# x read also in feature layout, its norm spread by small matmuls, and the modulation products moved to TensorE

## Chip, cores, metric

One core of one Trainium2 chip. The metric is the device time of one execution in microseconds, as the median of several runs. Engines are named as in the profile: PE (TensorE, matmuls), PEld (its weight loads), DVE (VectorE), ACT (ScalarE), POOL (GpSimd), SP (the engine that issues most DMAs).

## The reference, cut to what matters

```python
cond = jax.nn.silu(c)
mod = cond @ w_ada[l] + b_ada[l]                      # c: 1024, w_ada: 1024 x 3072
shift, scale, gate = jnp.split(mod, 3, axis=-1)
h = rmsnorm(x, norm_w[l]) * (1.0 + scale[:, None]) + shift[:, None]   # x: 2048 x 1024
u = h @ w_in[l]
a_x, a_g, hg_q, hg_f, hg_i, hg_g, ssd_z, ssd_xbc, ssd_dt = jnp.split(u, split_points, axis=-1)
...  # three branches: RG-LRU (ya), HGRN2 (yb), SSD (yc), each over 2048 tokens
y = jnp.concatenate([ya, yb, yc], axis=-1) @ w_out[l]
x = x + gate[:, None] * y
return rmsnorm(x, final_norm_w)
```

`rmsnorm(x, w)` is `x * rsqrt(mean(x*x, features) + eps) * w`.

## The kernel before

The 2048 tokens are cut into four blocks `tb` of 512 and the 1024 features into eight tiles `k` of 128. The normalised and modulated input is kept as eight `ht` tiles per block, 128 features by 512 tokens, each as a rounded high part and a low part (`hi`, `lo`), and each weight block likewise, so that one 128x512 projection tile is three matmuls. Blocks 0 and 1 are projected first (half 0), blocks 2 and 3 later (half 1).

*How an h tile is made.* `load_x` reads x as tokens by features. `norm_stats` squares it on ACT with a running sum, and takes root and reciprocal to `st`, one column per group of 128 tokens. `norm_scale` multiplies each x tile by its column of `st`, mostly on DVE. `h_tile` transposes four 128x128 pieces on PE (`ps_xt`), ACT applies scale and shift (`hf`, from the columns `gsc` of feature tile k), DVE rounds to the high part (a cast) and DVE or POOL subtracts for the low part.

*How `gsc` is made.* `mod_dma(j)` loads the shift and scale columns of w_ada that belong to feature tile j (`wta`). `mod_acc` multiplies and accumulates eight pieces on DVE into `macc`. `mod_col` sums `macc` over the partitions with a matmul by ones (`psm`), and DVE makes two columns of `gsc` in three small operations.

*The order of the opening* (blocks 0 and 1) is written by hand in a word list, `PROG`: D j loads, A j (part) multiplies, C j is `mod_col`, X loads x, S takes statistics, N scales x, H block k makes an h tile (a last `v` puts the low part on DVE instead of POOL), w and W load and split the first three weight blocks, M block k is nine matmuls of one h tile with them (`ps_f`, `ps_q`, `ps_g`), K makes constants, B starts the branches. PE runs in the order in which the code issues. A scheduler orders the other engines when the program is built, each engine then runs its queue strictly in order.

*The middle.* In the last pass of half 0 (loop index `i` 0 to 3; `ps_lx`, `ps_lg` are the projections of the RG-LRU, `ps_r`, `ps_i` its gate matmuls, `l_r` its scan, `l_gs` its output) x of block 2 is loaded at `i == 2` and scaled by the generator `norm_gen`; at `i == 3` x of block 3 is loaded and scaled in line, and `h_build(2)` makes block 2's h tiles between the projections. Half 1 starts with `ps_v` of block 2, woven with `h_build(3)`. Small tiles of 128x512 (`xt`, `xsq`, `macc`, `wta`, `raw`, `hf`) share 34 slots, so a load can wait until a slot is free.

Of the kernel before, what the change touches and what calls it, by code (L numbers as in the profile page):

```python
# [30 lines left out]
for _name, _w in (("norm_w", 8), ("b_shift", 8), ("b_scale", 8), ("c", 8),  # L31
# [13 lines left out]
LW, HGW = 2, 20  # L45
BW = (4, 1)
L0 = 0.01


@with_exitstack  # L50
def trunk(ctx, tc, x, w_ada, w_in, w_out, wa, wx, cols, rows, ident_in,
          tri_in, masks_in, onehot_in, out):
    nc = tc.nc
    V, S, G, PE = nc.vector, nc.scalar, nc.gpsimd, nc.tensor
# [11 lines left out]
    def act(o, i, f, **kw):  # L66
        S.activation(o, i, f, **kw)  # L67

    def tt(e, o, a, b, op):
        e.tensor_tensor(o, a, b, op=op)  # L70
# [212 lines left out]
    def norm_stats(xs):
        st = tmp("xst", (P, 2, 4), bufs=2)
        for n in range(2):
            for i in range(4):
                sq = tmp("xsq", (P, TB), BF16, bufs=1)
                act(sq, xs[i][n], AF.Square, accum_out=st[:, n, i:i + 1])
        tt(V, st[:, 0], st[:, 0], st[:, 1], ADD)
        sact(st[:, 0], st[:, 0], AF.Sqrt, scale=1.0 / D, bias=epsc[:, 0:1])  # L290
        V.reciprocal(st[:, 0], st[:, 0])
        return st

    def norm_scale(xs, st, n, on_act=()):
        for i in range(4):
            if on_act is G:
                tt(G, xs[i][n], xs[i][n], st[:, 0, i:i + 1].to_broadcast([P, TB]), MUL)
            elif i in on_act:
                act(xs[i][n], xs[i][n], AF.Copy, scale=st[:, 0, i:i + 1])
            else:  # L300
                V.tensor_scalar(xs[i][n], xs[i][n], st[:, 0, i:i + 1], None, op0=MUL)

    def norm_x(xs, on_act=()):
        st = norm_stats(xs)
        for n in range(2):
            norm_scale(xs, st, n, on_act)

    def h_tile(xs, k, dep=None, lo=G):
        ht = hp.tile([P, 2, TB], F32R, tag="h", name="ht")
        ps = bank(ps_ms, "ms", "ps_xt")  # L310
        for i in range(4):
            d_ = PE.transpose(ps[:, i * P:(i + 1) * P], xs[i][k // 4][:, (k % 4) * P:(k % 4 + 1) * P], ident)
# [3 lines left out]
        V.tensor_copy(ht[:, 0], hf)  # L316
# [112 lines left out]
    def mod_dma(j):  # L429
        mws[j] = []  # L430
        for q in range(4):
            wt = tmp("wta", (P, 2, 2, P))
            for s in range(2):
                nc.sync.dma_start(wt[:, :, s], w_ada[q * 256:(q + 1) * 256, s * D + j * P:s * D + (j + 1) * P]
                                  .rearrange("(k p) c -> p k c", p=P))
            mws[j].append(wt)

    def mod_acc(j, part):
        if part == 0:
            mas[j] = tmp("macc").rearrange("p (s c) -> p s c", c=P)  # L440
        ma = mas[j]
        for q in (2 * part, 2 * part + 1):
            wt = mws[j][q]
            for k in range(2):
                kk = 2 * q + k
                if kk == 0:
                    V.tensor_scalar(ma[:, 0:2], wt[:, k], cond[:, 0:1], None, op0=MUL)
                else:
                    stt(ma[:, 0:2], wt[:, k], cond[:, kk:kk + 1], ma[:, 0:2], MUL, ADD)

    def mod_col(j):
        ma = mas.pop(j)
        psm = bank(ps_ms, "ms", "psm")
        for i in range(2):
            PE.matmul(psm[:, i:i + 1], ma[:, i], ones[:, 0:1], start=True, stop=True)
# [444 lines left out]
    for half in range(2):  # L900
# [4 lines left out]
        for p in range(2):  # L905
# [26 lines left out]
            if half == 0 and p == 0:  # L932
# [100 lines left out]
        for i in range(4):  # L1033
# [214 lines left out]
```

## Time and profile before

| | us |
|---|---|
| median of 3 runs | 1797.67 (1796.58 to 1798.63) |
| span of the profiled execution | 1793.9 |
| PE busy in it | 1712.6 (95%) |
| DVE, POOL, ACT busy | 1138.6, 835.9, 627.3 |

The profiled execution's span stands 3.8 us under the median of the timed runs; the runs are about 1 us apart from each other. A row of the timeline reads: start, duration, engine, line of the kernel, operation, written tile `<-` read tiles, shapes, number of instructions, and in brackets the idle time of that engine ahead of it with what ended it. PE's fp32 matmuls show as two records each, and the ends of matmuls are modelled, so the distance from one start to the next is the better measure of a PE row. A row of the waits reads: engine, tile and line that waited, what it waited for, us in total, times, longest.

### The profile page before, as it was taken

What the parts mean: (1) busy time and instruction counts of PE and PEld (TensorE: products, weight loads), DVE (VectorE), ACT (ScalarE), POOL (GpSimd) and SP (SyncE); (2) the same over time, 40 slices, a digit from 0 to 9 for tenths busy, and PEclk for the clock granted to TensorE, in tenths of its full rate; (3) what the DMA queues carried; (4) which work ended last, traced back from release to release, by engine and by line L of the source; (5) the groups of instructions that cost most, each with busy time, mean ns of one, the idle gap of its engine ahead of it and who ended that gap; (6) DMA issues with size and microseconds to landing.
All of it is one profiled execution on the core that took longest, in us unless ns stands there. A gap on an engine that the chain in (4) does not pass through costs nothing. (4 is left out here: it accounts for less than half of the span.)

```text
span 1793.9 us, 29607 instructions
## 1 busy us (share of the span) xinstructions
PE 1712.6 (95%) x11448; PEld 1363.9 (76%) x11448; DVE 1138.6 (63%) x2340; ACT 627.3 (35%) x1188; POOL 835.9 (47%) x682
## 2 busy tenths in 40 slices
PE   3899999999999999899999999999999799999998
PEld 2688877777777777787877777777777577888886
DVE  6944657788877856815655778868759745333333
ACT  5322323233333357622322334333355632222221
POOL 3433334265635655524234346545567645333334
PEclk9899999999999999999999999999999999999999
DMA  8611011111202132321111002211234353333332
GB/s 249 176 37 48 25 37 37 36 36 48 71 24 57 51 109 82 82 65 31 43 43 37 25 27 57 57 39 36 58 96 131 115 159 119 96 96 95 95 95 69
DMA packets 178988, 129.51 MB, mean 72 GB/s; under 512 B 13856, under 2 KB 153632, under 8 KB 178848
## 3 DMA queue, kind: packets, MB, share of 16 engines
q1 hardware_dynamic: 142512, 102.72, 20.1%
q10 hardware_dynamic: 33936, 17.04, 3.2%
q0 software_dynamic: 2400, 7.87, 1.1%
q8 instruction: 90, 1.47, 0.3%
q14 instruction: 50, 0.41, 0.1%
HBM read 102.43 MB, written 25.17 MB: 71 GB/s over the span
## 5 line engine op out<-in xcount | busy, mean ns | idle before, releaser
L1087 PE MATMUL po<-wo,yy 128*128 128x512 f32 x1512 | 355.1, 397 | 3.2 <-POOL yy L70 2.5
L1087 PEld LDWEIGHTS po<-wo,yy 128*128 128x128 f32 x1512 | 285.1, 189 | 73.0 <-POOL yy L70 2.9
L70 POOL TENSOR_TENSOR w<-raw,w 128x512 fp32r<-128x512 f32 x158 | 225.1, 1444 | 218.3 <-ACT w L67 218.2
L73 DVE SCALAR_TENSOR_TENSOR cacc<-craw,col,cacc 128x512 f32<-128x512 f32 x192 | 199.3, 1038 | 2.0
L324 PE MATMUL ps_x<-ht,w 128*128 128x512 f32 x768 | 196.3, 403 | 0.0
L324 PE MATMUL ps_z<-ht,w 128*128 128x512 f32 x768 | 192.7, 401 | 0.0
L324 PEld LDWEIGHTS ps_x<-ht,w 128*128 128x128 f32 x768 | 139.2, 188 | 38.6 <-issue 10.7
L324 PEld LDWEIGHTS ps_z<-ht,w 128*128 128x128 f32 x768 | 140.9, 188 | 34.5 <-issue 4.1
L70 POOL TENSOR_TENSOR hg_k<-hg_k,hg_t 128x256 f32<-128x256 f32 x80 | 58.9, 736 | 192.5 <-PE ps_sB L579 70.5
L73 DVE SCALAR_TENSOR_TENSOR o<-po,rstd,o 128x512 f32<-128x512 f32 x64 | 47.5, 750 | 118.8 <-PE po L1087 110.5
L324 PE MATMUL ps_f<-ht,w 128*128 128x512 f32 x384 | 105.9, 415 | 6.2 <-DVE ht L316 5.8
L330 PE MATMUL ps_v<-vw,ht 128*128 128x264 f32 x768 | 105.5, 292 | 4.6 <-DVE ht L70 4.6
L67 ACT ACTIVATE w<-raw 128x512 fp32r<-128x512 f32 x158 | 91.4, 624 | 47.7 <-PE ps_q L324 29.5
L324 PE MATMUL ps_bc<-ht,w 128*128 128x512 f32 x384 | 107.2, 413 | 0.0
L324 PE MATMUL ps_q<-ht,w 128*128 128x512 f32 x384 | 105.8, 412 | 0.0
L330 PEld LDWEIGHTS ps_v<-vw,ht 128*128 128x128 f32 x768 | 97.1, 191 | 8.0 <-DVE ht L70 5.5
L324 PE MATMUL ps_lx<-ht,w 128*128 128x512 f32 x384 | 101.4, 416 | 0.0
L70 POOL TENSOR_TENSOR s_ce<-s_ce,cacc 128x512 f32<-128x512 f32 x64 | 98.1, 1552 | 3.1 <-ACT s_ce L67 2.7
L70 POOL TENSOR_TENSOR o<-o,gate 128x512 f32<-128x512 f32 x32 | 43.0, 1351 | 117.7 <-DVE o L70 112.5
L324 PE MATMUL ps_lg<-ht,w 128*128 128x512 f32 x384 | 94.2, 398 | 0.0
L324 PE MATMUL ps_g<-ht,w 128*128 128x512 f32 x336 | 92.4, 408 | 0.0
L70 POOL TENSOR_TENSOR yy<-yr,yy 128x512 fp32r<-128x512 f32 x61 | 78.4, 1308 | 26.3 <-ACT yy L67 25.9
(248 smaller groups left out, 3060.5 us busy)
## 6 DMA issues: line engine op xcount, KB each, us to landing
raw<-in_w_in SPq DMA_DIRECT2D x176, 256.0 KB, 3.2
yr<-yscr SPq DMA_DIRECT2D x64, 256.0 KB, 2.9
wta<-in_w_ada SPq DMA_DIRECT2D x64, 128.0 KB, 3.0
xt<-in_x SPq DMA_DIRECT2D x32, 256.0 KB, 5.0
yscr<-cacc ACTq DMA_DIRECT2D x32, 256.0 KB, 2.3
rawo<-in_w_out SPq DMA_DIRECT2D x32, 256.0 KB, 3.4
xr<-in_x SPq DMA_DIRECT2D x32, 256.0 KB, 3.1
out<-o POOLq DMA_DIRECT2D x30, 256.0 KB, 4.4
```

Source lines behind the costliest of these rows:

```text
L67: S.activation(o, i, f, **kw)
L70: e.tensor_tensor(o, a, b, op=op)
L73: V.scalar_tensor_tensor(o, a, s, b, op0=op0, op1=op1)
L324: d_ = PE.matmul(ps, b.hl[wl][:, k, :], ht[:, hl, :], start=(k == 0 and n == 0), stop=(k == KT - 1 and n == 2))
L330: d_ = PE.matmul(ps[:, 0:264], ht[:, hl, c * P:(c + 1) * P], b.vw[k // 4][wl][:, k % 4, :], start=(k == 0 and n == 0), stop=(k == KT - 1 a ...
L1087: PE.matmul(pss[t, n], yys[u, t][yl][:, k4, :], wts[4 * fam + k4][wl][n], start=(k4 == 0 and i == 0), stop=(k4 == 3 and i == 2))
```

## The change

- x is handed over a second time, transposed, as `x_t` (features by tokens), prepared outside the timed launch. `load_x` reads eight tiles of 128 features by 512 tokens. The PE transposes of `h_tile` are gone (128 in all).
- The sum of squares over features is now over partitions and tiles: `norm_sum` squares on ACT into eight `xsq` tiles and adds them in a row (on DVE in the opening, on POOL in `norm_gen`); `norm_cols` sums over partitions with four matmuls by ones (`ps_ss`) and takes root (ACT) and reciprocal (DVE); `norm_rows` spreads the four columns over all partitions with four matmuls against the identity (`ps_rb`) and copies them to `rb`.
- `h_pre` multiplies an x tile by `rb` on DVE and applies scale and shift on ACT, in place. `h_tile` is cast and subtraction alone.
- The modulation weights come in an order prepared outside (`w_mod`), 2 KB per partition and load; 32 loads of 256 KB replace 64 of 128 KB. `mod_mm` makes the products on PE: eight fp32 matmuls with `cond` padded by zeros to 32 columns, in four column tiles of the array, and an ACT copy to `macc`. The 64 DVE operations of `mod_acc` are gone.
- `PROG` is written anew. Block 0's h tiles come first, one per modulation column; R (norm columns and spread) stands ahead of each block's first H.
- `norm_gen` is in three pieces, and block 3's norm is a `norm_gen` behind `h_build(2)` instead of in line.

```diff
-PROG = ("D0 A00 X0 D1 A10 w0 A01 S0 X1 N0013 A11 C0 H00v W0 M00 D2 S1 C1 H01v N10 H10 A20 D3 w1 "
-        "A30 A21 A31 H11v M01 C2 D4 N111g H02 M10 H12 M11 W1 C3 N01 A40 H03 A41 D5 M02 H13 M12 C4 "
-        "A50 H04 D6 A51 M03 A60 H14 D7 M13 C5 H05 H15 A61 M14 M04 C6 K A70 H06 M05 A71 H16v M15 "
-        "C7 B H07v H17 M06 M07 M16 M17")
+PROG = ("X0 w0 D0 S0 D1 W0 w1 D2 R0 A0 W1 C0 H00 D3 A1 M00 C1 H01v D4 D5 A2 M01 C2 H02 X1 A3 M02 C3 H03v D6 D7 S1 "
+        "A4 M03 C4 H04 A5 M04 C5 H05v R1 H10 M10 A6 M05 C6 H06 H11v K M11 A7 M06 C7 H07v H12 M12 B M07 H13v M13 "
+        "H14 H15v M14 H16 M15 H17v M16 M17")
...
+    def norm_sum(xs, eng):
+        a = None
+        for k in range(KT):
+            sq = tmp("xsq")
+            act(sq, xs[k], AF.Square)
+            if a is None:
+                a = sq
+            else:
+                tt(eng, a, a, sq, ADD)
+        return a
+
+    def norm_cols(a):
+        ps = bank(ps_ms, "ms", "ps_ss")
+        for i in range(4):
+            PE.matmul(ps[:, i:i + 1], a[:, i * P:(i + 1) * P], ones[:, 0:1], start=True, stop=True)
+        st = tmp("xst", (P, 4), bufs=2)
+        sact(st, ps[:, 0:4], AF.Sqrt, scale=1.0 / D, bias=epsc[:, 0:1])
+        V.reciprocal(st, st)
+        return st
...
+    def norm_rows(st):
+        ps = bank(ps_ms, "ms", "ps_rb")
         for i in range(4):
...
+            PE.matmul(ps[:, i * P:(i + 1) * P], st[:, i:i + 1].to_broadcast([P, P]), ident, start=True, stop=True)
+        rb = tmp("rb")
+        act(rb, ps, AF.Copy)
+        return rb
+
+    def h_pre(xs, rb, k, eng=V):
+        tt(eng, xs[k], xs[k], rb, MUL)
+        act(xs[k], xs[k], AF.Identity, scale=gsc[:, 1, k:k + 1], bias=gsc[:, 0, k:k + 1])
 
     def h_tile(xs, k, dep=None, lo=G):
         ht = hp.tile([P, 2, TB], F32R, tag="h", name="ht")
-        ps = bank(ps_ms, "ms", "ps_xt")
-        for i in range(4):
-            d_ = PE.transpose(ps[:, i * P:(i + 1) * P], xs[i][k // 4][:, (k % 4) * P:(k % 4 + 1) * P], ident)
-            after(d_, dep)
-        hf = tmp("hf")
-        act(hf, ps, AF.Identity, scale=gsc[:, 1, k:k + 1], bias=gsc[:, 0, k:k + 1])
-        V.tensor_copy(ht[:, 0], hf)
-        tt(lo, ht[:, 1], hf, ht[:, 0], SUB)
+        after(V.tensor_copy(ht[:, 0], xs[k]), dep)
+        tt(lo, ht[:, 1], xs[k], ht[:, 0], SUB)
         return ht
...
+    def mod_mm(j):
+        psm = bank(ps_ms, "ms", "psm")
+        for k in range(KT):
+            r = k % 4
+            PE.matmul(psm[32 * r:32 * r + 32, 0:2 * P], condz[:, k, :], mws[j][k // 2][:, k % 2],
+                      start=k < 4, stop=k >= 4)
+        mas[j] = tmp("macc")
+        act(mas[j][:, 0:2 * P], psm[:, 0:2 * P], AF.Copy)
...
     def norm_gen(xs):
-        norm_x(xs)
+        a = norm_sum(xs, G)
+        yield
+        st = norm_cols(a)
+        yield
+        rb = norm_rows(st)
+        for k in range(KT):
+            h_pre(xs, rb, k)
         yield
...
             if i == 2 and half == 0:
                 xs_ = load_x(2)
-                pend += [(norm_gen(xs_), 1)]
+                pend += [(norm_gen(xs_), 3)]
...
                     xs_next = load_x(3)
-                    norm_x(xs_next)
                     HTS[2], HTS[3] = [None] * KT, [None] * KT
-                    hb = [(h_build(2, xs_, HTS[2], [h_use[id(t_)] for t_ in HTS[0]]), 8)]
+                    hb = [(h_build(2, xs_, HTS[2], [h_use[id(t_)] for t_ in HTS[0]]), 8), (norm_gen(xs_next), 3)]
```

Where instructions stand now, at three places. In the rows below `xN` at the end counts equal instructions in a row.

ACT's queue in the opening, before: statistics, two scalings of x, two weight splits, the first `hf`.

```order
L67 ACTIVATE xsq,xst<-xt 128x512 x8
L152 ACTIVATE xst<-xst,epsc 128x4
L67 ACTIVATE xt<-xt,xst 128x512 x2
L67 ACTIVATE w<-raw 128x512 x2
L67 ACTIVATE hf<-ps_xt,gsc 128x512
L67 ACTIVATE wt<-raw 128x512
L67 ACTIVATE xsq,xst<-xt 128x512 x8
```

The same queue after the change:

```order
L66 ACTIVATE xsq<-xt 128x512 x8
L66 ACTIVATE w<-raw 128x512
L66 ACTIVATE wt<-raw 128x512
L66 ACTIVATE w<-raw 128x512
L152 ACTIVATE xst<-ps_ss,epsc 128x4
L66 ACTIVATE w<-raw 128x512 x2
L66 ACTIVATE rb<-ps_rb 128x512
L66 ACTIVATE macc<-psm 128x256
L66 ACTIVATE wt<-raw 128x512
L66 ACTIVATE macc<-psm 128x256
L66 ACTIVATE xt<-xt,gsc 128x512 x2
```

The root now stands behind three splits, and the copy `rb` behind two more, whose weights (w1) are loaded later.

DVE's queue in the opening, before: two columns' products run around the scaling of x.

```order
L447 TENSOR_SCALAR macc<-wta,cond 128x256
L73 SCALAR_TENSOR_TENSOR macc<-wta,cond,macc 128x256
L291 RECIPROCAL xst<-xst 128x4
L73 SCALAR_TENSOR_TENSOR macc<-wta,cond,macc 128x256
L301 TENSOR_SCALAR xt<-xt,xst 128x512 x6
L73 SCALAR_TENSOR_TENSOR macc<-wta,cond,macc 128x256 x4
L316 CAST ht<-hf 128x512
```

The same place after the change:

```order
L69 TENSOR_TENSOR xsq<-xsq 128x512 x7
L300 RECIPROCAL xst<-xst 128x4
L69 TENSOR_TENSOR xt<-xt,rb 128x512 x8
L69 TENSOR_TENSOR gsc<-psm,col 128x1
L72 SCALAR_TENSOR_TENSOR gsc<-psm,col 128x1
L69 TENSOR_TENSOR gsc<-gsc,col 128x1
L317 CAST ht<-xt 128x512
```

All eight products of a block stand ahead of the first column `gsc` and the first cast.

POOL's queue in the middle, before: the recurrence's two outputs, then low parts of h tiles and weight splits.

```order
L70 TENSOR_TENSOR craw<-cacc 128x512 x2
L70 TENSOR_TENSOR craw<-craw,l_i 128x512 x2
L70 TENSOR_TENSOR l_gs<-l_r,l_gs 128x512 x2
L70 TENSOR_TENSOR ht<-hf,ht 128x512 x2
L70 TENSOR_TENSOR w<-raw,w 128x512
```

The same place after the change:

```order
L69 TENSOR_TENSOR craw<-cacc 128x512
L69 TENSOR_TENSOR ht<-xt,ht 128x512 x3
L69 TENSOR_TENSOR craw<-craw,l_i 128x512 x2
L69 TENSOR_TENSOR l_gs<-l_r,l_gs 128x512 x2
L69 TENSOR_TENSOR xsq<-xsq 128x512 x3
L69 TENSOR_TENSOR w<-raw,w 128x512
L69 TENSOR_TENSOR xsq<-xsq 128x512
L69 TENSOR_TENSOR w<-raw,w 128x512
L69 TENSOR_TENSOR xsq<-xsq 128x512 x3
```

Low parts now stand ahead of the recurrence's last steps, and block 3's seven sums behind them with two splits between.

PE at the same place, after the change (before, no norm matmul stood here, and every six projection matmuls were followed by four transposes `ps_xt`):

```order
L325 MATMUL ps_lg<-ht,w 128x512 x18
L297 MATMUL ps_ss<-ones,xsq 128x1 x4
L325 MATMUL ps_lg<-ht,w 128x512 x3
L306 MATMUL ps_rb<-ident,xst 128x128 x4
L325 MATMUL ps_lg<-ht,w 128x512 x3
L804 MATMUL ps_r<-cacc,wab 128x512
```

Block 3's column sum `ps_ss` and spread `ps_rb` stand in PE's order with the last projections of half 0 behind them.

More of the change, by code (lines that the diff above doesn't have):

```diff
@@ L50, in trunk @@
 @with_exitstack
-def trunk(ctx, tc, x, w_ada, w_in, w_out, wa, wx, cols, rows, ident_in,
+def trunk(ctx, tc, x, x_t, w_mod, w_gate, w_in, w_out, wa, wx, cols, rows, ident_in,
           tri_in, masks_in, onehot_in, out):
@@ L96, in trunk @@
     cond = cpool.tile([P, 8], F32, name="cond")
+    condz = cpool.tile([P, 8, 32], F32, name="condz")
     dhalf = cpool.tile([P, 8], F32, name="dhalf")
@@ L275, in load_x @@
     def load_x(tb):
-        r = [[tmp("xt") for _ in range(2)] for _ in range(4)]
-        for n in range(2):
-            for i in range(4):
-                r0 = tb * TB + i * P
-                nc.sync.dma_start(r[i][n], x[r0:r0 + P, n * TB:(n + 1) * TB])
-        return r
[L283 to L291, printed above, removed]
-        return st
@@ L294, in norm_scale @@
-    def norm_scale(xs, st, n, on_act=()):
+        r = []
+        for k in range(KT):
+            t_ = tmp("xt")
+            nc.sync.dma_start(t_, x_t[k * P:(k + 1) * P, tb * TB:(tb + 1) * TB])
+            r.append(t_)
+        return r
+    def norm_sum(xs, eng):
[8 more added lines that the diff above has]
+        return a
@@ L295, in norm_scale @@
+    def norm_cols(a):
[5 more added lines that the diff above has]
+        V.reciprocal(st, st)
+        return st
+    def norm_rows(st):
+        ps = bank(ps_ms, "ms", "ps_rb")
         for i in range(4):
[L296 to L306, printed above, removed]
+            PE.matmul(ps[:, i * P:(i + 1) * P], st[:, i:i + 1].to_broadcast([P, P]), ident, start=True, stop=True)
[5 more added lines that the diff above has]
+        act(xs[k], xs[k], AF.Identity, scale=gsc[:, 1, k:k + 1], bias=gsc[:, 0, k:k + 1])
     def h_tile(xs, k, dep=None, lo=G):
@@ L309, in h_tile @@
         ht = hp.tile([P, 2, TB], F32R, tag="h", name="ht")
-        ps = bank(ps_ms, "ms", "ps_xt")
-        for i in range(4):
-            d_ = PE.transpose(ps[:, i * P:(i + 1) * P], xs[i][k // 4][:, (k % 4) * P:(k % 4 + 1) * P], ident)
-            after(d_, dep)
-        hf = tmp("hf")
-        act(hf, ps, AF.Identity, scale=gsc[:, 1, k:k + 1], bias=gsc[:, 0, k:k + 1])
-        V.tensor_copy(ht[:, 0], hf)
-        tt(lo, ht[:, 1], hf, ht[:, 0], SUB)
+        after(V.tensor_copy(ht[:, 0], xs[k]), dep)
@@ L403, in trunk @@
     tt(V, cond, cond, cc("c", 0, 8), MUL)
+    G.memset(condz, 0.0)
+    V.tensor_copy(condz[:, :, 0:1], cond.unsqueeze(2))
     for half in range(2):
@@ L431, in mod_dma @@
         for q in range(4):
[L432 to L435, printed above, removed]
+            wt = tmp("wta", (P, 2, 2 * P))
+            nc.sync.dma_start(wt, w_mod[j, :, q * TB:(q + 1) * TB].rearrange("p (k c) -> p k c", k=2))
             mws[j].append(wt)
[L438 to L449, printed above, removed]
+    def mod_mm(j):
[6 more added lines that the diff above has]
+        act(mas[j][:, 0:2 * P], psm[:, 0:2 * P], AF.Copy)
     def mod_col(j):
@@ L454, in mod_col @@
         for i in range(2):
-            PE.matmul(psm[:, i:i + 1], ma[:, i], ones[:, 0:1], start=True, stop=True)
+            PE.matmul(psm[:, i:i + 1], ma[:, i * P:(i + 1) * P], ones[:, 0:1], start=True, stop=True)
         tt(V, gsc[:, 0, j:j + 1], psm[:, 0:1], cc("b_shift", j), ADD)
@@ L843, in gate_calc @@
             wt = tmp("wtg")
-            nc.sync.dma_start(wt, w_ada[k * P:(k + 1) * P, 2 * D + n * TB:2 * D + (n + 1) * TB])
+            nc.sync.dma_start(wt, w_gate[k * P:(k + 1) * P, n * TB:(n + 1) * TB])
             if k == 0:
@@ L861, in norm_gen @@
     def norm_gen(xs):
-        norm_x(xs)
+        a = norm_sum(xs, G)
[3 more added lines that the diff above has]
+        rb = norm_rows(st)
+        for k in range(KT):
+            h_pre(xs, rb, k)
         yield
@@ L944, in trunk @@
                     elif o_ == "A":
-                        mod_acc(*ar)
+                        mod_mm(ar[0])
                     elif o_ == "C":
@@ L950, in trunk @@
                     elif o_ == "S":
-                        sts[ar[0]] = norm_stats(xsb[ar[0]])
-                    elif o_ == "N":
-                        norm_scale(xsb[ar[0]], sts[ar[0]], ar[1], G if op_[-1] == "g" else ar[2:])
+                        sts[ar[0]] = norm_sum(xsb[ar[0]], V)
+                    elif o_ == "R":
+                        sts[ar[0]] = norm_rows(norm_cols(sts[ar[0]]))
                     elif o_ == "H":
+                        h_pre(xsb[ar[0]], sts[ar[0]], ar[1])
                         HTS[ar[0]][ar[1]] = h_tile(xsb[ar[0]], ar[1], None, e_)
@@ L1187, in trunk @@
     tc_pe.__exit__(None, None, None)
-_INS = ["x", "w_ada", "w_in", "w_out", "wa", "wx", "cols", "rows", "ident", "tri", "masks", "onehot"]
+_INS = ["x", "x_t", "w_mod", "w_gate", "w_in", "w_out", "wa", "wx", "cols", "rows", "ident", "tri", "masks", "onehot"]
 def _arrays(inp):
@@ L1223, in _arrays @@
         onehot[32 * n + np.arange(8), np.arange(8)] = 1.0
-    r = dict(x=g["x"][0], w_ada=g["w_ada"][0], w_in=g["w_in"][0], w_out=g["w_out"][0],
+    wada = g["w_ada"][0]
+    w_mod = wada[:, :2 * D].reshape(8, P, 2, 8, P).transpose(3, 1, 0, 2, 4).reshape(8, P, 2048)
+    r = dict(x=g["x"][0], x_t=g["x"][0].T, w_mod=w_mod, w_gate=wada[:, 2 * D:], w_in=g["w_in"][0], w_out=g["w_out"][0],
              wa=g["lru_wa"][0], wx=g["lru_wx"][0], cols=cols, rows=rows,
```

## The prediction

> **What bounds the kernel now.** I read the page's chain first, then the busy time by stretch, then the waits of the opening, then single rows. The chain names TensorE (PE) before anything else:
>
> ```profile
> PE 29%; DVE 3%; POOL 1%; DMA 1%; issue 1%; ACT 1%; SPq 0%; ACTq 0%; POOLq 0%; DVEq 0%
> ```
>
> A share over 1794 us hides where PE is idle, so the stretches come next (columns: length, then busy us of PE, PEld, DVE, ACT, POOL, granted clock, DMA share, GB/s):
>
> ```profile
> 0.00:90.00 90.00, 54.31 (x231) 42.13 (x232) 71.38 (x173) 39.56 (x78) 37.08 (x37) 0.91 0.76 212
> 90.00:1794.00 1704.00, 1658.29 (x11219) 1321.80 (x11217) 1067.19 (x2168) 587.79 (x1110) 798.87 (x646) 0.99 0.22 65
> 60.00:70.00 10.00, 8.93 (x46) 6.82 (x45) 9.89 (x30) 4.34 (x6) 3.36 (x3) 1.00 0.67 166
> 700.00:720.00 20.00, 16.06 (x69) 12.85 (x68) 14.31 (x19) 13.55 (x25) 11.17 (x10) 0.85 0.19 55
> 720.00:740.00 20.00, 18.57 (x106) 14.90 (x105) 15.89 (x27) 17.28 (x30) 11.94 (x10) 0.98 0.20 56
> 740.00:760.00 20.00, 14.83 (x106) 13.38 (x105) 18.88 (x27) 10.09 (x20) 9.98 (x7) 0.96 0.33 91
> ```
>
> Two places are open to this change. In the first 90 us PE is idle 35.7 us; VectorE (DVE) is busy 9.89 of 10 us there. At 700 to 760 us, where the second pair of token blocks is made, PE is idle 60 - 16.06 - 18.57 - 14.83 = 10.5 us. Elsewhere PE is full, so time is won or lost at these two places. What PE waits for in the opening:
>
> ```profile
> PE psm L455 <- DVE macc L73: 13.2, 4, 9.5
> PE ps_xt L312 <- DVE xt L301: 11.6, 5, 8.1
> PE ps_xt L312 <- DVE gsc L73: 4.7, 2, 4.2
> ```
>
> All three waits end on DVE. PE's rows of the opening give the pace:
>
> ```profile
> 25.47 0.79 PE L324 MATMUL ps_f<-ht,w 128*128 128x512 f32 x1 [5.81 <-DVE ht L316]
> 51.04 0.50 PE L455 MATMUL psm<-ones,macc 128*128 128x1 f32 x4
> 57.42 0.58 PE L455 MATMUL psm<-ones,macc 128*128 128x1 f32 x4 [0.76 <-DVE macc L73]
> 81.43 1.12 PE L312 MATMUL ps_xt<-ident,xt 128*128 128x128 f32 x4 [4.19 <-DVE gsc L73]
> 82.19 1.63 PE L324 MATMUL ps_f<-ht,w 128*128 128x512 f32 x3
> 88.12 0.85 PE L324 MATMUL ps_f<-ht,w 128*128 128x512 f32 x3
> 88.81 0.86 PE L324 MATMUL ps_q<-ht,w 128*128 128x512 f32 x3
> 92.39 0.65 PE L568 MATMUL ps_sA<-hg_q,hg_k 128*32 128x64 f32 x32
> ```
>
> The first projection starts at 25.47, the opening ends at 92.39, and one modulation column serves two h tiles every 57.42 - 51.04 = 6.4 us. Three projection matmuls take 88.81 - 88.12 = 0.69 us, so one h tile's nine take 2.1 us.
>
> **The change, opening.** The costs that I use:
>
> ```profile
> L73 DVE SCALAR_TENSOR_TENSOR macc<-wta,cond,macc 128x256 f32<-128x256 f32 x56 | 38.8, 692 | 1.9 <-DMA wta<-in_w_ada 0.9
> L447 DVE TENSOR_SCALAR macc<-wta,cond 128x256 f32<-128x256 f32 x8 | 2.8, 344 | 0.7 <-DMA wta<-in_w_ada 0.7
> L70 DVE TENSOR_TENSOR ht<-hf,ht 128x512 fp32r<-128x512 f32 x5 | 3.4, 682 | 0.0
> L316 DVE CAST ht<-hf 128x512 fp32r<-128x512 f32 x16 | 6.7, 419 | 1.1 <-ACT hf L67 1.1
> L70 DVE TENSOR_TENSOR gsc<-psm,col 128x1 f32<-128x1 f32 x8 | 1.2, 152 | 2.8 <-PE psm L455 2.8
> L67 ACT ACTIVATE hf<-ps_xt,gsc 128x512 f32<-128x512 f32 x16 | 12.1, 777 | 31.0 <-issue 11.5 <-DVE gsc L70 10.6 <-PE ps_xt L312 8.7
> L67 ACT ACTIVATE xsq<-xt 128x512 bf16<-128x512 f32 x16 | 10.1, 629 | 5.5 <-DMA xt<-in_x 5.1
> ```
>
> Removed: 38.8 + 2.8 = 41.6 us of DVE, and 64 PE transposes. Added: 14 sums and 16 products of 128x512 on DVE at 0.63 to 0.68 us (20 us), 16 scalings on ScalarE (ACT) in place of the 16 `hf`, and on PE eight groups of modulation products. DVE thus has 20 us less to do. What decides is the length of the chain.
>
> Modulation product: eight fp32 matmuls of 256 columns. The nearest rows:
>
> ```profile
> 154.34 1.05 PE L624 MATMUL ps_kv<-hg_v,hg_kt 128*128 128x128 f32 x8
> 155.15 1.64 PE L324 MATMUL ps_g<-ht,w 128*128 128x512 f32 x6
> 113.53 0.65 PE L568 MATMUL ps_sA<-hg_q,hg_k 128*32 128x64 f32 x32
> ```
>
> Eight records (four fp32 matmuls of 128 columns) take 155.15 - 154.34 = 0.81 us, so eight of 256 columns take 3.2 us one after another. The third row is the only column-tiled one: 32 records of 64 columns would take 1.6 us by that pace and take 0.6. So 1.2 us if the tiles overlap as there, 3.2 if they do not; I take 1.2, the same kind of tile. The Trainium skill, "TensorE: Matmul & The Clock Gate", part 3 (Measured speedup vs the span model), gives 2.38x for three column tiles, which would make it 3.2/2.38 = 1.3 us, an estimate by that page. The trace's 2.7x agrees roughly, so the sum would stand.
>
> *First h tile.* It needs norm, modulation column, scaling and cast. ACT's queue now holds the second pair of weight splits ahead of the copy `rb`; they wait for data that SP issues behind 8 x, 3 weight and 8 modulation loads of 256 KB each, 5 MB in. Before, 8 x loads of 256 KB and 16 modulation loads of 128 KB, 4 MB, stood ahead of the first split, which could start at 19.70:
>
> ```profile
> 19.70 1.38 ACT L67 ACTIVATE w<-raw 128x512 fp32r<-128x512 f32 x2 [0.68 <-DMA raw<-in_w_in]
> 51.75 1.48 POOL L70 TENSOR_TENSOR ht<-hf,ht 128x512 fp32r<-128x512 f32 x1
> 52.13 1.38 DVE L73 SCALAR_TENSOR_TENSOR macc<-wta,cond,macc 128x256 f32<-128x256 f32 x1
> ```
>
> Modulation rows of 2 KB instead of 512 B help, so I take 20 us for the landing. Then splits 1.38, `rb` 0.63, all eight products `xt<-xt,rb` in DVE's queue ahead of the first column (8 x 0.63 = 5.0, plus about 1.0, since DVE takes 1.38 us beside a GpSimd (POOL) operation, the last two rows), three column operations 0.45, scaling 0.78, cast 0.42: first projection at 29.6, 4.1 us later than before.
>
> *Block 0, words M00 to M04.* Each h tile is now a serial chain: column 0.36, three operations 0.45, scaling 0.78, cast 0.42, the low part 0.68 (DVE) or 1.48 (POOL), the remaining seven matmuls 1.6, handoffs 0.3: 4.6 or 5.4 us. The next A (1.2) fits under scaling and cast. Four steps are 20 us, half clock in the first adds 1.7, and X1's eight squares ahead of A4's copy in ACT's queue add about 2.5: M04 starts at 53.8 and ends at 57.
>
> *R1.* PE runs nothing while the column sums 0.72, root and reciprocal 0.5, spread 0.81, copy 0.63, all eight products 5.0, scaling 0.78, cast 0.42 and handoffs 0.6 pass: M10 at 66.5. Then M10 3.2, A6 1.2, M05 2.1, C6 0.4, a gap of 2.5 (column to cast, two casts), M11 2.4, A7 1.2, M06 2.1, C7 0.4, gap 2.5, M12 3.2, six tiles at 2.1: 33.8, and 1.7 for half clock after the idle time. The opening ends near 102, **+9.6 us**. Ends: +3 (loads at the best rate, no half clock), +16 (half clock through block 0 too).
>
> **The change, middle.** Before, PE and POOL:
>
> ```profile
> 681.55 11.37 PE L324 MATMUL ps_lg<-ht,w 128*128 128x512 f32 x48
> 696.02 1.02 PE L808 MATMUL ps_i<-cacc,wab 128*128 128x512 f32 x2
> 707.35 0.60 PE L312 MATMUL ps_xt<-ident,xt 128*128 128x128 f32 x4
> 707.71 1.64 PE L324 MATMUL ps_lx<-ht,w 128*128 128x512 f32 x6
> 715.12 1.11 PE L312 MATMUL ps_xt<-ident,xt 128*128 128x128 f32 x4 [3.94 <-ACT hf L67]
> 715.89 2.91 PE L324 MATMUL ps_lx<-ht,w 128*128 128x512 f32 x6
> 690.48 1.30 POOL L70 TENSOR_TENSOR l_gs<-l_r,l_gs 128x512 f32<-128x512 f32 x1 [3.40 <-DVE l_r L830]
> 716.71 1.28 POOL L70 TENSOR_TENSOR l_gs<-l_r,l_gs 128x512 f32<-128x512 f32 x1 [1.16 <-DVE l_r L830]
> ```
>
> Block 2's column sum now stands in PE's order 18 matmuls (4.2 us) after `ps_lg` begins. It waits for seven POOL sums of 1.3 us, which stand around the second `l_gs` of the recurrence. That one ended 690.48 + 1.30 - 681.55 = 10.2 us after `ps_lg` began; with six sums behind it PE would stall 10.2 + 7.8 - 4.2 = 13.8. Without it, squares 1.6 and seven sums 9.1 leave 6.5. I take 10, since DVE no longer scales x ahead of that recurrence. Behind the stalled sum stand all of PE's later projections.
>
> Block 3's column sum stands 87 matmuls (20.3 us) after the second `ps_i`. It waits for both `l_gs`, which by the rows end 716.71 + 1.28 - 697.04 = 21.0 us after that `ps_i`, then for seven sums with two weight splits between them (9 x 1.3 = 11.7): 12.4 us of stall. Four low parts of block 2 now stand in POOL's queue ahead of the recurrence, 5.2 us more. Between 12.4 and 19 I take 17.6, because those four sit in the chain.
>
> Against this: the 10.5 us idle of before go; 16 x (707.71 - 707.35) = 5.8 us of transposes go; two spreads and column sums cost 2 x (0.81 + 0.72) = 3.1 on PE. After the one idle time of 3.94 us the next rows took 1.11 and 2.91 instead of 0.60 and 1.64, 1.8 us of half clock; two long stalls make that twice, +1.8. Sum: 10 + 17.6 - 10.5 - 5.8 + 3.1 + 1.8 = **+16.2 us**; ends +7 and +21. DVE and ACT hide their norm work under these stalls, and SP's loads of block 3, which wait for the slots of block 2's squares, land while the recurrence still runs. The Trainium skill, "TensorE: Matmul & The Clock Gate" (HAM oscillation), warns of any PE gap over about 3.4 us; the row after 3.94 us agrees, and with its half rate the restart would cost an estimated 1.7 us, which leaves the sum.
>
> The output projection and the gate's loads change names only: nothing.
>
> **Sum.** 9.6 + 16.2 = 25.8. The profiled execution spans 1793.9 us, the median of the runs is 1797.67; the difference carries over to the median: 1823.5, taken as 1823. About 0.2% (3.6 us) is what a measurement of this kernel can tell from no change.
>
> **Rivals.**
> - *DVE was the bound, and freeing it wins* (faster). For: the three waits of the opening, 29.5 us, all end on DVE. PE's work there is 16 x 2.1 + 8 x 1.2 + 8 x 0.4 + 3 = 49 us; started at 25.5 with no gap it ends at 75, -17. It decides if an h tile's chain stays under the 3.7 us of work that PE has per tile; by the rows it is 4.6 to 5.4. With the middle at its low end, +7, 1788; 0.08.
> - *The sums in the middle land in time* (loads and squares run ahead): middle -5 instead of +16, 1802. Against: block 2's squares stand behind the last `ps_lx` copy in ACT's queue; 0.11.
> - *Column tiles do not overlap, or the opening stays at half clock*: 8 x 2.0 us more, half of it under ACT and DVE, or +7 for half clock: 1832; 0.16.
>
> **Chances.** Forecast (both places late) 0.65. Faster 0.08, within 0.2% 0.05 (the second rival at its low end), slower 0.87. Likeliest range 1813 to 1833; the cases beside it stretch it to 1803 to 1838.
>
> **What would show it.** First projection at 29 to 30 us and `rb` near 22; M10 after a PE gap of 8 to 10 us; `ps_sA` first at 98 to 106. In the middle, two PE gaps before `ps_ss`, released by POOL `xsq`, of 7 to 14 and 12 to 19 us; no gaps on `hf`. Modulation groups at 1.2 us. Wrong if `ps_ss` does not wait, or if block 0 runs faster than 4 us per tile.

## The result, and the profile after

The changed kernel takes 1849.22 us (median of 4 runs, 1848.09 to 1850.82) against 1797.12 for the kernel before in the same runs: ratio 1.0289, 95% interval 1.0274 to 1.0303. It is slower, as forecast, by 52 us where the prediction had 26; its range ended at 1838. The profiled execution spans 1848.9 us (before 1793.9), so 55.0 us are to be found.

First the busy time by stretch (columns as before):

```profile
0.00:90.00 90.00, 48.60 (x244) 33.91 (x244) 38.92 (x112) 31.98 (x56) 16.91 (x21) 0.77 0.59 188
760.00:780.00 20.00, 0.00 (x0) 0.00 (x0) 13.41 (x13) 9.59 (x15) 15.02 (x12) 0.53 0.38 105
```

DVE's busy time in the opening fell from 71.4 to 38.9 us, as the change intends, and PE did less there, not more: 48.6 us of work for 54.3, at a mean granted clock of 0.77 for 0.91. In the middle PE does nothing for 20 whole us. The waits of PE, first those of 0 to 125 us, then those of 690 to 840 us:

```profile
PE ps_f L325 <- DVE ht L317: 20.5, 8, 6.0
PE ps_ss L297 <- DVE xsq L69: 14.2, 1, 14.2
...
PE ps_ss L297 <- POOL xsq L69: 37.3, 2, 24.6
PE ps_v L331 <- DVE dtr L366: 5.8, 1, 5.8
```

PE's rows date the two places (start, duration, what ended the gap ahead):

```profile
31.98 0.79 PE L325 MATMUL ps_f<-ht,w 128*128 128x512 f32 x1 [5.86 <-DVE ht L317]
46.47 0.86 PE L325 MATMUL ps_q<-ht,w 128*128 128x512 f32 x3
50.31 0.50 PE L325 MATMUL ps_f<-ht,w 128*128 128x512 f32 x1 [0.94 <-DVE ht L317]
51.91 1.48 PE L325 MATMUL ps_q<-ht,w 128*128 128x512 f32 x3
57.75 0.56 PE L325 MATMUL ps_f<-ht,w 128*128 128x512 f32 x1 [1.69 <-DVE ht L317]
62.68 0.85 PE L452 MATMUL psm<-ones,macc 128*128 128x1 f32 x4
74.26 0.79 PE L325 MATMUL ps_f<-ht,w 128*128 128x512 f32 x1 [6.02 <-DVE ht L317]
78.98 1.07 PE L443 MATMUL psm<-wta,condz 128*32 128x256 f32 x16
79.99 0.96 PE L325 MATMUL ps_f<-ht,w 128*128 128x512 f32 x3
114.57 0.65 PE L565 MATMUL ps_sA<-hg_q,hg_k 128*32 128x64 f32 x32
705.28 4.37 PE L325 MATMUL ps_lg<-ht,w 128*128 128x512 f32 x18
722.36 1.86 PE L297 MATMUL ps_ss<-ones,xsq 128*128 128x1 f32 x8 [12.70 <-POOL xsq L69]
736.66 1.02 PE L805 MATMUL ps_i<-cacc,wab 128*128 128x512 f32 x2
782.55 1.86 PE L297 MATMUL ps_ss<-ones,xsq 128*128 128x1 f32 x8 [24.63 <-POOL xsq L69]
806.75 17.36 PE L331 MATMUL ps_v<-vw,ht 128*128 128x264 f32 x120 [5.78 <-DVE dtr L366]
823.94 11.26 PE L325 MATMUL ps_f<-ht,w 128*128 128x512 f32 x48
```

The kernel before reaches the row after `ps_v`, the first long `ps_f` of half 1, here:

```profile
769.15 11.26 PE L324 MATMUL ps_f<-ht,w 128*128 128x512 f32 x48
```

Two marks cut every run into three parts: the first `ps_sA` ends the opening, the long `ps_f` ends the middle. Opening 114.57 against 92.39, +22.2; from there to the `ps_f` 709.4 against 676.8, +32.6; the rest 1025.0 against 1024.8. Both places lost, and nothing else moved. The marks are of one profiled execution each. The changed kernel, mod_pe, all_mm_c, hyb_mm and hyb_late were timed 4 to 10 times, the other versions once; fast runs of the kernel before lie between 1795.3 and 1799.5. All runs by these marks, in us (the rest varied from 1022.8 to 1025.2 without a pattern):

| kernel | opening ends | to the long `ps_f` | time |
|---|---|---|---|
| before | 92.4 | 676.8 | 1797.1 to 1798.6 |
| changed | 114.6 | 709.4 | 1849.2 |
| mid_old | 114.2 | 675.9 | 1816.7 |
| open_old | 92.5 | 708.5 | 1826.4 |
| mod_pe | 85.4 | 678.4 | 1788.9 |
| mid_dve | 113.5 | 700.6 | 1840.0 |
| mid_mm | 112.1 | 679.7 | 1816.6 |
| mid_late | 115.5 | 706.1 | 1848.6 |
| fill | 109.3 | 708.1 | 1842.1 |
| open_ord | 107.3 | 707.9 | 1841.1 |
| all_mm | 109.4 | 680.0 | 1814.6 |
| all_mm_c | 90.6 | 680.0 | 1795.7 |
| hyb_mm | 83.3 | 681.0 | 1788.6 |
| hyb_late | 84.6 | 690.4 | 1800.9 |

### The profile page after: what moved, and what is told of

Read it like the earlier page. It is cut to its first block, busy times and chain, and to the rows that moved or that the text cites. A ratio compares the mean times of both kernels' runs of the same rounds, so it can differ in the third digit from the quotient of the medians.

```text
span 1848.9 us, 29610 instructions
## 1 busy us (share of the span) xinstructions
PE 1725.7 (93%) x11512; PEld 1371.3 (74%) x11512; DVE 1129.2 (61%) x2296; ACT 623.9 (34%) x1164; POOL 848.8 (46%) x690
## 5 line engine op out<-in xcount | busy, mean ns | idle before, releaser
L325 PEld LDWEIGHTS ps_f<-ht,w 128*128 128x128 f32 x384 | 70.1, 193 | 47.2 <-DVE ht L317 23.7
L69 POOL TENSOR_TENSOR o<-o,gate 128x512 f32<-128x512 f32 x32 | 43.0, 1350 | 118.7 <-DVE o L69 113.5
```

Of the source, the lines that this page charges most:

```text
L325: d_ = PE.matmul(ps, b.hl[wl][:, k, :], ht[:, hl, :], start=(k == 0 and n == 0), stop=(k == KT - 1 and n == 2))
```

## The experiments

### Taking the change apart: mid_old, open_old, mod_pe

*mid_old* is the changed kernel with blocks 2 and 3 made the old way: `load_x`, `norm_x` and `h_tile` of the kernel before stand beside the new ones.

```diff
-                xs_ = load_x(2)
-                pend += [(norm_gen(xs_), 3)]
+                xs_ = load_x_o(2)
+                pend += [(norm_gen(xs_), 1)]
```

> The changed kernel with blocks 2 and 3 made as before (x as tokens, transposes, norm without PE), the opening as changed. Theory (two places add up: the opening costs 22 us, the middle 31): 1849 - 31 = 1818 us, the two waits of PE on the sums gone, idle time of 700 to 800 us back near 10 us. Rival (the late opening shifts the later work so that the middle stalls anyway, or the middle's cost is the opening's in another place): within 5 us of 1849.

*open_old* is the reverse, the kernel before with blocks 2 and 3 made the new way.

> The kernel before with only blocks 2 and 3 made in the new way; opening, modulation on DVE and word list as before. Theory (places add up): 1797 + 31 = 1828 us, with PE waits on the POOL sums of about 12 and 24 us. Rival (the middle stalls only because the opening came late or left other slots): near 1800.

*mod_pe* is the kernel before with one part of the change: the modulation products on PE (`w_mod`, `mod_mm`), the order and the transposes as they were.

```diff
-                        mod_acc(*ar)
+                        if ar[1] == 1:
+                            mod_mm(ar[0])
```

> The kernel before with one part of the change alone: modulation products on PE in column tiles, loads in 2 KB rows; x, norm, transposes and word list as before. Theory (the products on PE are no loss, freeing DVE of 41.6 us is a gain, and the loss of the opening comes from the serial chain with x in features): 1787 to 1793 us, opening ends 4 to 10 us earlier than 92.4. Rival (the products on PE, their copies and half clock are what the opening lost): 1800 to 1808.

Measured: 1816.66 and 1826.35. The two places add up: the spans are 21.0 and 30.4 us over the 1793.9 of before, 51.4 of the 55.0. PE's waits at 690 to 840 us go with the way in which blocks 2 and 3 are made. The longest of mid_old:

```profile
PE ps_xt L358 <- ACT hf L66: 4.4, 2, 3.9
```

And those of open_old, which are the changed kernel's:

```profile
PE ps_ss L342 <- POOL xsqn L70: 37.4, 2, 24.7
PE ps_v L376 <- DVE dtr L411: 4.2, 1, 4.2
```

mod_pe took 1788.91 us, ratio 0.9947 (0.9930 to 0.9963): this part alone is a gain of half a percent. Its first 90 us:

```profile
0.00:90.00 90.00, 70.35 (x459) 49.39 (x460) 44.45 (x121) 46.41 (x96) 39.21 (x40) 1.00 0.72 218
```

DVE fell to 44.5 us there, much as in the changed kernel, but PE did 70 us of work. The mean clock of 1.00 in this row can't hold for every matmul: the triple at 24.50 us took 1.48 us, as the triples at half clock of the changed kernel do, so the rows of PE are the better witness of half clock than this column. So freeing DVE does help; what lost the time is x as features, with its norm and its order, taken together.

### The middle: mid_dve, mid_mm, mid_late

*mid_dve* moves the sums of squares of blocks 2 and 3 from POOL to DVE: `a = norm_sum(xs, V)`.

> The changed kernel with the sums of squares of blocks 2 and 3 on DVE (0.69 us each) instead of POOL (1.3 to 1.7). Theory (the waits are the sums themselves plus their place behind the recurrence): first wait 12.7 to about 6, second 24.6 to about 16, total near 1834 us. Rival (the waits are the recurrence and ACT's queue alone, the sums only end last): no change, 1847 to 1851.

Measured 1840.03. The two waits of `ps_ss` fell to 9.2 and 21.8 us, only 6.4 together and less than the theory had: the engine of the sums is the smaller part of them.

*mid_mm* takes the sums and the small spread away altogether. Eight matmuls with a matrix of ones sum the rounded squares over features and spread the sum in one go.

```diff
-        a = norm_sum(xs, G)
-        yield
-        st = norm_cols(a)
-        yield
-        rb = norm_rows(st)
+        sqs = [...]                         # ACT: squares, rounded type
+        yield
+        ps = bank(ps_ms, "ms", "ps_rb")
+        for k in range(KT):
+            PE.matmul(ps, onesr, sqs[k], start=(k == 0), stop=(k == KT - 1))
+        rb = tmp("rb")
+        sact(rb, ps, AF.Sqrt, scale=1.0 / D, bias=epsc[:, 0:1])
+        V.reciprocal(rb, rb)
```

> The changed kernel, but the norm of blocks 2 and 3 (not of the opening) without POOL: the squares are written rounded, and eight matmuls with a matrix of ones sum and spread them straight into the bank of rb; ScalarE takes the root, VectorE the reciprocal over 128x512. The column sums, the small spread and POOL's seven sums go. Theory (stall 1 is the sum on POOL, stall 2 is the sum on POOL plus the queue ahead of the squares): the first wait of 12.7 us falls to under 2, the second of 24.6 to about 10 since the squares still stand behind the second transposition-free block's queue; time about 1825. Rival (the products and tiles of block 3 behind the norm set the end whatever the sum costs): at least 1840.

Measured 1816.6, 32.6 us less, and more than expected. PE's rows at the two norms, and the squares that the second one waits for:

```profile
706.99 2.03 PE L870 MATMUL ps_rb<-xsq,onesr 128*128 128x512 f32 x8
719.13 1.02 PE L805 MATMUL ps_i<-cacc,wab 128*128 128x512 f32 x2
751.50 4.44 PE L870 MATMUL ps_rb<-xsq,onesr 128*128 128x512 f32 x8 [11.11 <-ACT xsq L66]
...
750.82 2.19 ACT L66 ACTIVATE xsq<-xt 128x512 fp32r<-128x512 f32 x4 [3.21 <-POOL l_gs L69]
```

The first wait is gone: it hung on POOL's sums, most of which stood behind the recurrence's second `l_gs` in POOL's queue. The second is 11.1 instead of 24.6, so 13.5 us of it went with the sums and splits behind the recurrence. The rest is the recurrence: block 3's squares stand in ACT's queue behind the store of `l_gs`, 750.82 - 719.13 = 31.7 us after the second `ps_i` began. The third wait, on `dtr`, still took 3.1 + 1.2 us. So 29.7 of the middle's 32.6 us come back; the features layout with a short norm gains nothing there and still costs about 3 us (679.7 against 676.8 of before).

*mid_late* leaves the sums as they were and moves block 3's column sum and spread to the first passes of half 1, behind work that needs nothing of block 3.

```diff
-                    brs = pend + [(h_build(tbs[1], xs_next, HTS[tbs[1]], hdep[tbs[1]]), 8)]
+                    brs = pend + [(norm_rest(xs_next, a_next), 2), (h_build(tbs[1], ...), 8)]
```

> The changed kernel, but block 3's column sums, spread and products stand no longer on TensorE's queue ahead of half 1's first passes: they are woven into them, ahead of block 3's tiles. The sums stay where they were, on POOL. Theory (the second wait of 24.6 us is a matter of the place in TensorE's order: 24 us of ps_v of block 2 stand right behind it and depend on nothing of block 3): the wait falls to under 8, and the kernel to 1829 to 1837. Rival (the wait only moves to ps_v of block 3, whose tiles come that much later): gain under 6, 1843 or more.

Measured 1848.57: nearly no gain. The rival was right in the sum, though not in the place. PE's waits at 690 to 840 us:

```profile
PE ps_ss L297 <- POOL xsq L69: 14.4, 2, 12.7
PE ps_r L804 <- DVE cacc L72: 12.6, 1, 12.6
PE ps_rb L306 <- DVE xst L300: 6.9, 1, 6.9
PE ps_v L331 <- DVE l_gs L69: 3.8, 1, 3.8
```

The 24.6 us became 1.7 + 12.6 + 6.9 + 3.8 = 25.0 (the wait on `dtr` went). The 12.6 us are the recurrence in another place: the next gate matmul `ps_r` needs `cacc`, which DVE computes from a copy of `ps_lx` by ACT, and that copy (773.15 in this trace) stands in ACT's queue behind the stores of `l_gs` and block 3's last squares. `ps_r` starts at 780.41. A second try of the same move on a better base, hyb_late below, meets the same wait.

### The opening: fill, open_ord, all_mm, all_mm_c

*fill* adds matmuls that nothing reads in two gaps, ahead of the first projection and behind block 1's spread, to keep PE's clock up.

> The changed kernel with matmuls that nothing reads in two gaps of the opening: three of 128x512 ahead of the first projection, 24 of the rounded type behind block 1's spread; they write a bank that is started anew later. Theory (the half clock behind the gaps costs the opening 4 to 6 us of the 22 that it lost): the triples behind both gaps run at 0.85 us and not at 1.48, and the opening ends 3 to 5 us sooner, about 1845. Rival (the arrival of h tiles sets the pace, and half clock fills time that would be waited anyway): the triples are shorter, the end stays within 1.5 us, 1847.5 to 1850.

Measured 1842.14, and the opening ends 5.3 us sooner. Its first 90 us:

```profile
0.00:90.00 90.00, 56.13 (x303) 38.25 (x303) 39.50 (x116) 33.32 (x59) 16.89 (x21) 0.91 0.62 194
```

And PE's rows: a triple of M00, the triple that answers to 51.91 above (M03), and one of block 1's first tile:

```profile
34.08 1.49 PE L325 MATMUL ps_q<-ht,w 128*128 128x512 f32 x3
52.69 0.86 PE L325 MATMUL ps_q<-ht,w 128*128 128x512 f32 x3
71.98 0.85 PE L325 MATMUL ps_q<-ht,w 128*128 128x512 f32 x3
```

Work that does nothing made the kernel faster: the last two triples take 0.86 and 0.85 us, and 1.48 each in the changed kernel (51.91 and 76.62). Half clock lay on the path. But behind the first filler M00 still ran at half clock (34.08: 1.49 us), so the expectation held for the second gap alone; why M03 and M04 ran at full clock here is not shown. By the end of M04 the run was 2.2 us ahead, at block 1's first projection 3.3, at the end of the opening 5.3; the two fillers were not run apart. The mean clock is still at 0.91.

*open_ord* moves two words of `PROG`: block 0's spread ahead of the weight splits, block 1's ahead of A5 and M04.

```diff
-X0 w0 D0 S0 D1 W0 w1 D2 R0 A0 W1 C0 ... A4 M03 C4 H04 A5 M04 C5 H05v R1 H10 M10
+X0 w0 D0 S0 D1 R0 W0 w1 D2 A0 W1 C0 ... A4 M03 C4 H04 R1 A5 M04 C5 H05v H10 M10
```

> The changed kernel with two places of the opening's order moved: block 0's spread ahead of the first weight halves' splits, and block 1's column sums and spread ahead of the modulation group of column 5 and of the projections' sixth step. Theory (rb of block 0 stood behind the splits on ScalarE, 22.65 where its bank was full at 18.7; block 1's chain from 62.7 to 74.3 stood alone on TensorE): first projection near 29, the first of block 1 no longer behind a gap of its own; the opening ends 8 to 11 us sooner, 1838 to 1841. Rival (VectorE's tiles or the weights' arrival set the pace behind it): less than 3 us sooner.

Measured 1841.07, opening 7.2 us sooner, a little under the 8 to 11 expected. Three rows of ACT and PE:

```profile
18.04 0.60 ACT L66 ACTIVATE rb<-ps_rb 128x512 f32<-128x512 f32 x1 [2.38 <-PE ps_rb L306]
29.55 0.79 PE L325 MATMUL ps_f<-ht,w 128*128 128x512 f32 x1 [4.47 <-DVE ht L317]
65.57 0.79 PE L325 MATMUL ps_f<-ht,w 128*128 128x512 f32 x1 [2.19 <-DVE ht L317]
```

`rb` is copied 4.6 us sooner (22.65 in the changed kernel), the first projection starts 2.4 sooner, and block 1's first at 65.57 instead of 74.26, with a gap of 2.2 us for 6.0.

*all_mm* uses the ones matmuls of mid_mm for all four blocks, with block 0's norm ahead of the splits, as in open_ord, and block 1's squares later (S1 behind H04).

> The changed kernel with the norm of all four blocks by eight matmuls of the rounded squares with a matrix of ones (as in mid_mm), no sums on VectorE or POOL and no small spread; block 0's norm ahead of the weight splits and block 1's ahead of the sixth column step, as in open_ord; block 1's squares a little later, since they hold eight tiles. If the parts add (1816.6 of mid_mm, 8 less by open_ord's order) 1808; VectorE's 14 sums of 0.69 go, and the reciprocal over 128x512 costs 3.35 twice, so the opening's two chains get a few us shorter: 1802 to 1808. Rival (the reciprocal of 3.35 stands on VectorE ahead of products and tiles and gives it back): 1808 to 1814.

Measured 1814.61: missed. In the kernel that ran, block 1's norm stood where the change has it, not where the expectation's words put it, so that a gap remained ahead of block 1:

```profile
27.68 0.79 PE L353 MATMUL ps_f<-ht,w 128*128 128x512 f32 x1 [3.19 <-DVE ht L345]
68.44 0.80 PE L353 MATMUL ps_f<-ht,w 128*128 128x512 f32 x1 [9.44 <-DVE ht L345]
14.74 3.35 DVE L327 RECIPROCAL rb<-rb 128x512 f32<-128x512 f32 x1 [10.85 <-ACT rb L152]
```

The reciprocal over 128x512 takes 3.35 us where the four columns took 0.2; the first projection still starts 1.9 us before that of open_ord.

*all_mm_c* goes on from all_mm: each modulation column (A, C) and h tile stands one step ahead of the projections that it used to follow, and block 1's norm stands ahead of M05.

```diff
-A0 W1 C0 H00 D3 A1 M00 C1 H01v D4 D5 A2 M01 C2 H02 X1 A3 M02 C3 H03v ...
+A0 W1 A1 C0 H00 D3 A2 C1 H01v M00 D4 D5 A3 C2 H02 X1 M01 A4 C3 H03v M02 ...
```

> As all_mm, and each modulation column (group on TensorE, copy, sum, shift and scale) one step earlier in the order, so that its chain of four engines no longer starts when the projections of the step before end. Theory (in the opening of the changed kernel steps 0 to 4 took 5 to 7.6 us each, though their nine matmuls and one group take 3.6 at full clock: the chain column, activation, cast stood behind each): 6 to 12 us less than all_mm, 1792 to 1802. Rival (the loads of the modulation weights and of x set the pace of these steps): within 3 us of all_mm.

Measured 1795.71, ratio 0.9998 (0.9989 to 1.0008): the whole loss is gone. PE's rows of steps 1 and 2, and block 1's first:

```profile
35.52 0.94 PE L353 MATMUL ps_f<-ht,w 128*128 128x512 f32 x3
39.24 0.94 PE L353 MATMUL ps_f<-ht,w 128*128 128x512 f32 x3
...
63.41 0.79 PE L353 MATMUL ps_f<-ht,w 128*128 128x512 f32 x1 [5.60 <-DVE ht L345]
```

Steps 1 and 2 take 3.7 us each with no wait, against a mean of (57.75 - 31.98)/4 = 6.4 in the changed kernel. Block 1's first tile still waits 5.6 us and then 3.9 for its low part, and the opening ends 5 us behind that of mod_pe. The new place of the columns and that of block 1's norm were not run apart.

### The part that gains, with the new middle: hyb_mm, hyb_late

*hyb_mm* is mod_pe with blocks 2 and 3 from x as features and the norm of mid_mm.

> mod_pe (the kernel before with the modulation products on TensorE alone), and blocks 2 and 3 from x as features with the norm by ones matmuls (mid_mm). The middle of mid_mm took 118.7 - 32.6 = 86.1 us where the kernel before took 87.6, so about 1787 if the parts add. Rival (VectorE's reciprocals of 3.35 and the f32 casts weigh more where the opening is shorter): 1789 to 1793.

Measured 1788.61, ratio 0.9954 (0.9940 to 0.9969), between its two expectations and no better than mod_pe's 1788.91: the new layout adds nothing that can be measured. What is left to win seemed to be its 11.1 us wait ahead of block 3's norm. *hyb_late* moves that norm into half 1, as mid_late did.

> As hyb_mm, and block 3's ones matmuls woven into half 1's first passes rather than ahead of them (as in mid_late). In mid_late the wait moved to ps_r and to the norm's own chain of sum, root, small spread; here that chain is one step. Theory (what is left of the second wait, 11.1 us in mid_mm, is the place in TensorE's order): 1777 to 1783. Rival (the chain of the recurrence gives the same end wherever the norm stands, as in mid_late): 1785 to 1788.

Measured 1800.85, 12 us slower than hyb_mm, slower than the kernel before, and outside both expectations. In the middle PE waited 11.1 us for `xsq` and 5.2 for `dtr` in hyb_mm, 16.3 together. Here it is 12.6 for `cacc`, 2.7 for `l_gs`, 8.8 for DVE's queue and 1.5 for `ht`, 25.6 together. The two longest waits, with DVE's queue ahead of the second:

```profile
733.23 2.08 PE L850 MATMUL ps_r<-cacc,wab 128*128 128x512 f32 x2 [11.19 <-DVE cacc L73]
...
751.25 1.88 DVE L70 TENSOR_TENSOR xt<-xt,rb 128x512 f32<-128x512 f32 x3
...
754.24 4.14 DVE L70 TENSOR_TENSOR xt<-xt,rb 128x512 f32<-128x512 f32 x5
758.64 0.15 DVE L412 COPY dtr<-ps_v 128x8 f32<-128x8 f32 x1
758.87 0.78 PE L377 MATMUL ps_v<-vw,ht 128*128 128x264 f32 x2 [8.76 <-DVE lcar L874]
```

So the rival was right about the first wait: taken out of PE's order, the 11.1 us ahead of the norm came back as 11.2 us ahead of the gate matmul `ps_r`, which needs the end of the same recurrence, as in mid_late. The second wait grew from 5.2 to 8.8 us. The 0.15 us copy `dtr`, which frees the bank that PE's next `ps_v` needs, stands in DVE's queue behind the norm's eight products. (The profile names `lcar`, the copy right behind it, which ends at 758.86; in hyb_mm it names `dtr` for this wait. That `dtr` is what counts here too is inferred.) The work that was to cover the norm hung on the same queue as the norm.

## Why the prediction was right or wrong

**Sign and places: right.** Both places lost, PE waits on `xsq` as said, and everything else stayed (1.5 us up to the middle, 0.2 behind it). The modulation group takes 79.99 - 78.98 = 1.0 us at full clock; 1.2 was taken, 3.2 would be no overlap. So the third rival fails on its column tiles, and is half right on the clock.

**The steps that failed.** In the opening it is the term for half clock, 1.7 us charged twice, and with it smaller terms of the first tile. In the middle it is the sentence that "DVE and ACT hide their norm work under these stalls": DVE's queue made the recurrence 5.9 us later than forecast and PE stall a third time, 5.8 us that had no term.

**Opening: 9.6 forecast, 22.2 measured.** By the prediction's own steps:

| step | forecast | measured |
|---|---|---|
| `rb` copied, end | 22.0 | 23.2 |
| first projection | 29.6 | 31.98 |
| M04 starts, ends | 53.8, 57 | 57.75, 62.7 |
| first projection of block 1 | 66.5 | 74.26 |
| from there to the end | 35.5 | 40.3 |

The steps came in the order forecast, and each took longer. The first projection was 2.4 us late, 1.2 of it because `rb` was, 1.0 because the eight products took 7.04 us in place of 6.0:

```profile
23.26 7.04 DVE L69 TENSOR_TENSOR xt<-xt,rb 128x512 f32<-128x512 f32 x8 [6.63 <-DMA wta<-in_w_mod]
```

(The profile puts the idle time ahead of them down to a load; the copy `rb`, which they read, ended at 23.23.)

Half clock was charged 1.7 us twice, behind the first tile and behind R1. In the trace it also came back in M03 and M04 (51.91: 1.48 us, behind gaps of only 0.9 and 0.2 us), and R1's own spread ran at it (2.08 us, 1.16 in fill). fill, which left M00 at half clock, won 5.3 us, where the prediction had charged 1.7 for all half clock behind M00. The prediction tied half clock to one long gap; here it came back with no gap over 0.94 us since 39.55. The gaps alone do not decide it, though: in fill the triple of M03 took 0.86 us behind gaps of 2.15 and 0.71. What sets the moment stays open. The Trainium skill, "TensorE: Matmul & The Clock Gate" (A second HAM failure mode: psum-queue depth-cycling), describes this form too, in a kernel that cycles through PSUM banks: a PE that idles briefly and often between groups of matmuls and so swings between half and full rate; this trace agrees that the rate swings, with 0.86 against 1.48 us for the same triple at 46.47 and 51.91. Of the 12.6 us that were missing, the 2.4 of the first projection and 3.6 of half clock (5.3 - 1.7) are shown; no run assigns the remaining 6.6.

The first rival's condition was a chain under 3.7 us. For this order it was rightly dismissed, since a step took 6.4 us. But the chain was taken as a length, when it was also a place in the order: all_mm_c issues it a step ahead, and its steps 1 and 2 run in 3.7 us.

**Middle: 16.2 forecast, 31.1 measured from `ps_lg`** (118.7 us from 705.28 to 823.94, before 87.6 from 681.55 to 769.15).
- Stall 1: 10 forecast, 12.70 measured, within its ends (6.5 and 13.8) and near the upper one, which is what happened: six of the seven sums stand behind the recurrence's second `l_gs` (first row below) and end 713.57 + 8.73 - 705.28 = 17.0 us after `ps_lg` began, 4.4 of which `ps_lg` covers.
- Stall 2: 17.6 forecast, 24.63 measured, over its upper end of 19. The recurrence and the sums were the right terms; the 5.2 us for low parts in POOL's queue named the wrong queue. The other rows show it:

```profile
713.57 8.73 POOL L69 TENSOR_TENSOR xsq<-xsq 128x512 f32<-128x512 f32 x6
756.88 1.72 POOL L69 TENSOR_TENSOR ht<-xt,ht 128x512 fp32r<-128x512 f32 x1 [1.90 <-DVE ht L317]
758.91 0.63 ACT L152 ACTIVATE craw<-craw 128x512 f32<-128x512 f32 x1 [10.94 <-DVE craw L820]
768.47 1.27 POOL L69 TENSOR_TENSOR l_gs<-l_r,l_gs 128x512 f32<-128x512 f32 x1 [1.16 <-DVE craw L513]
778.56 3.94 POOL L69 TENSOR_TENSOR xsq<-xsq 128x512 f32<-128x512 f32 x3
```

  The recurrence ended (768.47 + 1.27) - (736.66 + 1.02) = 32.1 us after the second `ps_i` did. 21.0 + 5.2 = 26.2 was forecast, the 5.2 for four low parts of block 2 in POOL's queue. But POOL itself stood idle ahead of the last of them, until DVE's cast came: DVE's queue held block 2's casts and low parts too and ran without a gap from 743.3 to 758.9, and ACT waited 10.94 us for DVE's `craw`. That is +5.9; the sums took 782.50 - 769.74 = 12.8 instead of 11.7, +1.1.
- A third stall, 5.78 us on `dtr`, was not foreseen: eight products of block 3 and most of the work on its eight tiles stand ahead of that copy on DVE (788.27 to 806.54). hyb_late shows the same queue doing the same.

The three excesses, 2.7 + 7.0 + 5.8 = 15.5, cover the 14.9 that were missing (31.1 - 16.2), with 0.6 to spare.

**The range.** Both places went past their own upper ends, 22.2 against 16 and 31.1 against 21. In the middle the stalls hung on the same queue of DVE, and were late together.

## What to carry to other kernels

Before moving work off a busy engine, write down what the new steps stand behind in each queue and what stands behind them: here the gain (modulation products on PE, about -9 us) was real, and short serial chains placed in PE's strict order cost some 60 (1849.2 against 1788.9). A chain over four engines need not be shortened if the order issues it one step ahead of the work that covers it, but cover counts only if it does not itself need the queue on which the chain runs. Where a sum over partitions must be spread again, one group of matmuls by ones replaces sums, column matmuls and spread at once.

## What was not expected of the hardware

- Work without use made the kernel faster: 27 idle-time matmuls raised the mean granted clock of the first 90 us from 0.77 to 0.91, and the opening ended 5.3 us sooner (one run; the whole was 7.1 us shorter, but behind both marks alone the versions differ by 2 us without a pattern).
- Short gaps do not decide alone when PE falls to half clock: the same triple of M03 took 1.48 us behind gaps of 0.94 and 0.22, and 0.86 behind 2.15 and 0.71 in fill. Open remains what does, and how much of the opening's loss is half clock in all: fill filled two gaps, not every one.
